# Output projection of a two-layer decoder: column blocks 2 and 3 done together, with two seven-product quads over the MLA heads

## The chip, the core and the metric

The kernel runs on one core of one Trainium2 chip. The metric is the device time of one execution in microseconds. Its engines are TensorE (PE in the profile, its weight loads PEld), VectorE (DVE), ScalarE (ACT), GpSimd (POOL) and SyncE (SP); loads are issued from SP's queue, accumulating transfers from GpSimd's.

## What is computed

Two layers over 256 tokens of width 2048. Each has a sparse attention (8 heads, "A") and an MLA attention (8 heads, "B") side by side, one output projection over both, a norm, and a SwiGLU FFN with a second norm. What the change touches is the last line of the mixer and the residual:

```
mix = einsum('bse,ed->bsd', concatenate([out_a, out_b], -1), w_o)   # 256 x 2048 by 2048 x 2048
x   = layer_norm(ALPHA * x + mix, ln1_g, ln1_b)
```

## The kernel before

Every product of fp32 data is made of three matmuls in a reduced fp32 format: both operands are split into a high and a low part (`split`, L427: ScalarE copies the high part, VectorE subtracts it for the low one), and high x high, high x low and low x high go into one PSUM bank (`proj`, L378, lines 392 to 394). Weights come in units of 256 rows by 512 columns (two 128-row pieces side by side, 128x1024 on chip, 512 KB): `load_raw` issues the load from SP's queue into one of four raw buffers, `parts` (L360) splits it into one of five pairs wh/wl. A unit serves both halves of the tokens (t = 0 and 1, 128 each) with two pieces and three matmuls, 12 matmuls of 128x512.

The projection's rows are 16 pieces: 0 to 7 are the A heads, 8 to 15 the B heads (`olhs`, L935). Its columns are four blocks of 512. For each block, `proj` runs over six units (`first`, L939: 8, 10, 12, 14, 0, 2), into two banks, one for each half of the tokens, and VectorE adds them into x (L944). The last two A units (4 and 6) are left for `last_pass` (L951): after the last attention heads it takes each half of the tokens over all four blocks, adds into x (L974), and as soon as a half is complete spawns its norm (`norm_T`: bn_stats L439, bn_aggr L441, a power on GpSimd L445, bnnb L451, normalization on ScalarE L460, transposes on PE, scaling on ScalarE L469, cast and low part on VectorE L472 and L473). Its eight units are split ahead, four of them into tiles named "many" and "own". The FFN's first matmuls need the first half's norm.

Beside the projection run, as generators that are stepped once a unit (`tick`), the last two sparse attention pairs (their outputs oA are split by VectorE) and `presums` (L844): sums of FFN weights on VectorE (tile q, L863 to L867), written back to HBM by GpSimd's queue for later. The FFN already uses a scheme of seven products for a 2x2 block of products (`gate_up`): sums and differences of weights on VectorE, and of activations ("few", "many"), in place of the eighth product.

There are eight PSUM banks: 0 to 3 for `acc`, 4 and 5 for transposes (`trp`), 6 and 7 as one pair (`att`). The framework's scheduler puts the instructions in their final order on each engine; each engine then runs in that order.

## Time and profile before

| | us |
|---|---|
| median of 3 runs | 2135.92 |
| lowest, highest | 2135.21, 2136.48 |
| profiled execution | 2134.82 |
| its span, first to last instruction | 2133.0 |

A row of the timeline has the start in us from the span's start, the duration, the engine, the line, the operation, output <- inputs, the shape and a count, and in brackets how long the engine had been idle and what ended that. Equal rows that follow each other are merged, so a duration with a count is that of the run. A row of the windows has the stretch, its length, and the busy time and number of instructions (x) of each engine. Layer 0's projection starts at 285 us, layer 1's at about 1347. Lines of the profile are those of the kernel before.

### The profile page before, as it was taken

The page shows a single profiled execution, that of the slowest core. Times are in us where ns is not written, and L with a number is a line of the kernel's source. Part 1 is how long each engine was busy: PE and PEld are TensorE (multiplying, and loading weights), DVE is VectorE, ACT ScalarE, POOL GpSimd, SP SyncE. Part 2 cuts the span into 40 slices and gives each one's busy share as a digit, 9 for nine tenths or more (in the row PEclk, how much of TensorE's full clock was granted, in tenths as well). Part 3 has the DMA queues.
Part 4 walks back from the last instruction along what each step waited for, and adds up shares of the span by engine and source line. Part 5 has one row for each costly group of instructions (what it writes and reads, how often), then busy time and mean ns, then how long its engine had stood idle before and what let it go on. Part 6 is the DMA issues. An engine that isn't in the chain of part 4 may idle for free.

```text
span 2133.0 us, 28390 instructions
## 1 busy us (share of the span) xinstructions
PE 2119.3 (99%) x9894; PEld 1760.1 (83%) x9894; DVE 1860.1 (87%) x2359; ACT 1334.7 (63%) x1714; POOL 330.9 (16%) x527
## 2 busy tenths in 40 slices
PE   9999999999999999999999999999999999999998
PEld 8888888888878888888888888888888888888886
DVE  7696776899999999999867976778999999999997
ACT  6556654766666666766655566547666666666773
POOL 1222220011111110110012232201111111110111
PEclk9999999999999999999999999999999999999999
DMA  8688888588888989987657889885989988988984
GB/s 311 207 298 292 309 298 309 183 239 263 247 257 272 286 279 291 281 264 254 217 172 247 302 292 290 324 279 186 253 258 243 289 262 276 285 277 292 282 300 118
DMA packets 175439, 564.49 MB, mean 265 GB/s; under 512 B 30928, under 2 KB 31232, under 8 KB 174656
## 3 DMA queue, kind: packets, MB, share of 16 engines
q1 hardware_dynamic: 110736, 398.38, 52.1%
q0 software_dynamic: 51600, 160.77, 29.4%
q10 hardware_dynamic: 12960, 3.54, 1.1%
q8 instruction: 77, 1.26, 0.2%
q14 instruction: 66, 0.54, 0.1%
HBM read 506.51 MB, written 31.46 MB: 252 GB/s over the span
## 4 chain that ended last, share of the span: by engine, by line
PE 88%; DVE 7%; issue 2%; DMA 1%; ACT 1%; POOL 0%; SPq 0%; DVEq 0%; ACTq 0%; POOLq 0%
PE acc L392 9%; PE acc L393 9%; PE acc L394 9%; PE acc L1186 7%; PE acc L1187 7%; PE acc L1185 7%; PE gu_p L1068 6%; PE gu_p L1071 6%; PE gu_p L1070 6%; DVE wl L429 3%; PE gu_c L1068 3%; PE gu_c L1071 3%; PE gu_c L1070 3%; PE tr L425 2%; PE att L1068 2%
## 5 line engine op out<-in xcount | busy, mean ns | idle before, releaser
L428 ACT ACTIVATE wh<-raw 128x1024 fp32r<-128x1024 f32 (+2 forms) x925 | 948.1, 1050 | 538.0 <-PE acc L394 128.1
L429 DVE TENSOR_TENSOR wl<-raw,wh 128x1024 fp32r<-128x1024 f32 (+2 forms) x925 | 1090.3, 1212 | 186.2 <-ACT wh L428 184.1
L392 PE MATMUL acc<-wh,xhl 128*128 128x512 f32 (+1 forms) x756 | 296.9, 393 | 0.0
L394 PE MATMUL acc<-wh,xhl 128*128 128x512 f32 (+1 forms) x756 | 292.1, 387 | 0.0
L393 PE MATMUL acc<-wl,xhl 128*128 128x512 f32 (+1 forms) x756 | 291.7, 386 | 0.0
L1186 PE MATMUL acc<-wl,hT 128*128 128x512 f32 x640 | 249.6, 390 | 0.9 <-DVE wl L429 0.8
L1185 PE MATMUL acc<-wh,hT 128*128 128x512 f32 x640 | 250.3, 392 | 0.0
L1187 PE MATMUL acc<-wh,hT 128*128 128x512 f32 x640 | 249.4, 390 | 0.0
L392 PEld LDWEIGHTS acc<-wh,xhl 128*128 128x128 f32 x756 | 142.0, 188 | 30.2 <-issue 3.3
L394 PEld LDWEIGHTS acc<-wh,xhl 128*128 128x128 f32 x756 | 141.9, 188 | 27.2
L393 PEld LDWEIGHTS acc<-wl,xhl 128*128 128x128 f32 x756 | 142.1, 188 | 26.5 <-DVE wl L429 1.2
L1186 PEld LDWEIGHTS acc<-wl,hT 128*128 128x128 f32 x640 | 120.2, 188 | 27.0 <-DVE wl L429 2.8
L1187 PEld LDWEIGHTS acc<-wh,hT 128*128 128x128 f32 x640 | 120.1, 188 | 25.1
L1185 PEld LDWEIGHTS acc<-wh,hT 128*128 128x128 f32 x640 | 120.2, 188 | 24.3
L1194 POOL DMA_DIRECT2D x<-d x80 | 68.1, 855 | 425.1 <-ACT d L1193 424.0
L1070 PE MATMUL gu_c<-wl,xhl 128*128 128x512 f32 x336 | 130.9, 390 | 0.1
L1071 PE MATMUL gu_c<-wh,xhl 128*128 128x512 f32 x336 | 130.7, 389 | 0.0
L1068 PE MATMUL gu_c<-wh,xhl 128*128 128x512 f32 x336 | 130.7, 389 | 0.0
L1193 ACT ACTIVATE d<-acc 128x512 f32<-128x512 f32 x80 | 47.7, 596 | 75.8 <-PE acc L1187 75.8
L1070 PE MATMUL gu_p<-wl,many 128*128 128x512 f32 x240 | 93.5, 390 | 0.0
L1068 PE MATMUL gu_p<-wh,many 128*128 128x512 f32 x240 | 93.4, 389 | 0.0
L1071 PE MATMUL gu_p<-wh,many 128*128 128x512 f32 x240 | 93.4, 389 | 0.0
(309 smaller groups left out, 3847.2 us busy)
## 6 DMA issues: line engine op xcount, KB each, us to landing
raw<-in_w_gate_dram SPq DMA_DIRECT2D x176, 512.0 KB, 5.6
raw<-in_w_down_dram SPq DMA_DIRECT2D x176, 512.0 KB, 8.2
raw<-in_w_in_dram SPq DMA_DIRECT2D x144, 512.0 KB, 5.6
sum<-in_w_up_dram POOLq DMA_DIRECT2D x124, 512.0 KB, 7.5
raw<-in_w_up_dram SPq DMA_DIRECT2D x100, 512.0 KB, 5.7
raw<-in_w_o_dram SPq DMA_DIRECT2D x64, 512.0 KB, 6.2
q<-q POOLq DMA_DIRECT2D x56, 512.0 KB, 5.0
raw<-q SPq DMA_DIRECT2D x56, 512.0 KB, 5.8
```

The lines of the kernel that those rows point to most:

```text
L392: mm(o[t][:, :n], h, a, start=first, stop=False)
L393: mm(o[t][:, :n], h, b, start=False, stop=False)
L394: mm(o[t][:, :n], l, a, start=False, stop=final)
L428: high = nc.scalar.activation(hi, src, AF.Copy)
L429: nc.vector.tensor_tensor(lo, src, f(hi), op=ALU.subtract)
L1068: mm(o[name], h, a, start=name not in begun, stop=False)
L1070: mm(o[name], h, b, start=False, stop=False)
L1071: mm(o[name], l, a, start=False, stop=end)
L1185: mm(o[c][t], h, wh[:, j, :], start=begin, stop=False)
L1186: mm(o[c][t], h, wl[:, j, :], start=False, stop=False)
L1187: mm(o[c][t], lo, wh[:, j, :], start=False, stop=end)
L1194: nc.gpsimd.dma_start(xt[t][:, c * C:(c + 1) * C], d, accum_op=ALU.add)
```

## The change

Blocks 0 and 1 go on as before. Blocks 2 and 3 become one stage, `col_pair`: first the A units 0 and 2 plainly for both blocks, into four banks (c11 and c21 are block 2's for the two token halves, c12 and c22 block 3's), then, once the attention is done, two quads. A quad takes the B units 8 and 12 (then 10 and 14), of both columns, for both token halves: seven products of six matmuls instead of eight. Four weight tiles r11, r12, r21, r22 are loaded; VectorE makes four sums of them in place; sums and differences of the heads' outputs (`head_sums`, spawned ahead of block 1) are the other operands. p6 and p7 get a transpose bank each, p1 and p5 the pair. After the second quad c22, c11, c12 and c21 go into x as before, the rest through four differences in small buffers, of which GpSimd's queue adds four into x by accumulating transfers.

```diff
+        places = ((8, 12), (10, 14))
+
+        def head_sums():
...
+            for u, v in places:
+                few = t8([P, 4, 2, KU, P], F32R, "hsum")
...
+                    nc.vector.tensor_tensor(w, f(hi), f(lo), op=ALU.add)
...
+                    nc.vector.tensor_tensor(w, y, z, op=ALU.subtract)
+                    split(few[:, i, 0], few[:, i, 1], w)
...
+                a21 = o(1, u)
+                s1 = diff(0, a21, o(1, v))
+                a11 = o(0, u)
+                s2 = diff(1, a11, s1)
+                diff(2, a21, a11)
+                diff(3, o(0, v), s2)
+                yield 1
...
+        def col_pair(cols, ks, sums):
...
+            finish(*a)
+            (c11, c21), (c12, c22) = (o[c] for c in cols)
+            p6, p7, p15 = trp(), trp(), att()
...
+            into(1, 1, c22)
+            for q, (u, v) in enumerate(places):
+                final = q == len(places) - 1
+                two = t8([P, 2, KU * C], F32, "wsum")
+                r11, r12 = two[:, 0], two[:, 1]
...
+                r21, r22 = (load_raw(w_o[l, c, v // KU], KU * C) for c in cols)
...
+                product(p1, token(0), r11, u, begin, final)
...
+                        nc.scalar.activation(e0, p1, AF.Copy)
+                product(c11, token(0), r21, v, False, final)
+                if final:
+                    into(0, 0, c11)
+                    added(0, 0, e0)
+                tick()
+                nc.vector.tensor_tensor(r12, r12, r22, op=ALU.add)
+                product(c12, summed("s4"), r22, u, False, final)
+                if final:
+                    into(0, 1, c12)
+                nc.vector.tensor_tensor(r11, r12, r11, op=ALU.add)
+                product(p6, summed("s2"), r11, u, begin, final)
+                if final:
+                    e1 = less(e0, p6)
+                tick()
+                nc.vector.tensor_tensor(r21, r11, r21, op=ALU.add)
+                product(p7, summed("s3"), r12, u, begin, final)
+                if final:
+                    e2 = less(e1, p7)
+                nc.vector.tensor_tensor(r22, r11, r22, op=ALU.subtract)
+                product(c21, token(1), r21, v, False, final)
+                if final:
+                    into(1, 0, c21)
+                    added(1, 0, e2)
+                tick()
+                product(p5, summed("s1"), r22, u, begin, final)
+                if final:
+                    for t, e in ((0, e1), (1, e2)):
+                        added(t, 1, less(p5, e))
+                tick()
...
-        for c in range(D // C):
+        for c in range(2):
+            if c:
+                spawn(held(head_sums(), head))
             o = proj([(w_o[l, c, k // KU], range(k, k + KU)) for k in first], olhs, C)
...
+        col_pair((2, 3), (0, 2), head)
+        turns["acc"] = 2
         finish(*a)
```

`into` is VectorE's scalar_tensor_tensor of ALPHA * x + bank (L1001 of the changed kernel), `less` its difference of two tiles or banks (L1006), `added` the accumulating transfer (L1010), `product` splits a weight tile and issues the six matmuls.

How the instructions move is shown at two places on VectorE in layer 0. The first is after block 0's eviction into x. Before, the rows are that eviction (x, acc), low parts of block 1's third to sixth units (wl), presums (q) and an attention output (oA):

```order
L944 SCALAR_TENSOR_TENSOR x1_66<-x1_66,acc658_2999 128x512
L944 SCALAR_TENSOR_TENSOR x2_67<-x2_67,acc659_3000 128x512
L429 TENSOR_TENSOR wl735_3286<-raw733_3283,wh734_3285 128x1024
L866 TENSOR_TENSOR q669_3045<-q673_3067,q669_3045 128x1024
L867 TENSOR_TENSOR q692_3125<-q673_3067,q692_3125 128x1024
L429 TENSOR_TENSOR wl738_3306<-raw736_3303,wh737_3305 128x1024
L429 TENSOR_TENSOR oA454_2189<-tr723_3235,oA453_2188 128x512
L429 TENSOR_TENSOR wl743_3328<-raw741_3325,wh742_3327 128x1024
L429 TENSOR_TENSOR wl748_3350<-raw746_3347,wh747_3349 128x1024
```

In the change the same eviction is followed by 24 small operations of the head sums (av, sv, hsum), with block 1's third unit, the two attention outputs and the presums among them; this is how that stretch ends, and the fourth unit's low part (wl756) stands behind it:

```order
L952 TENSOR_TENSOR av744_3298<-oB314_1589,oB315_1590 128x256
L866 TENSOR_TENSOR q669_3045<-q673_3067,q669_3045 128x1024
L429 TENSOR_TENSOR hsum737_3279<-sv742_3290,hsum737_3279 128x256
L957 TENSOR_TENSOR sv745_3300<-av744_3298,sv742_3290 128x256
L429 TENSOR_TENSOR oA454_2189<-tr750_3326,oA453_2188 128x512
L429 TENSOR_TENSOR hsum737_3279<-sv745_3300,hsum737_3279 128x256
L867 TENSOR_TENSOR q692_3125<-q673_3067,q692_3125 128x1024
L429 TENSOR_TENSOR wl756_3356<-raw754_3353,wh755_3355 128x1024
L429 TENSOR_TENSOR wl761_3378<-raw759_3375,wh760_3377 128x1024
```

Block 1's fourth unit (wl738 before, wl756 now) has moved from the sixth row to behind 31 rows.

The second place is the end of the blocks 2 and 3. Before, it is the last units of block 3, the weights of the last pass (own, wl) and the evictions:

```order
L429 TENSOR_TENSOR wl788_3574<-raw786_3571,wh787_3573 128x1024
L429 TENSOR_TENSOR wl793_3599<-raw791_3596,wh792_3598 128x1024
L429 TENSOR_TENSOR own799_3616<-raw803_3623,own799_3616 128x1024
L429 TENSOR_TENSOR wl797_3609<-raw795_3606,wh796_3608 128x1024
L429 TENSOR_TENSOR own804_3627<-raw808_3634,own804_3627 128x1024
```

In the change it is the second quad: weight sums (wsum, and raw in place), low parts of its products (wl), a weight of the last pass (many), evictions (L1001) and differences (we):

```order
L1050 TENSOR_TENSOR wsum803_3578<-wsum803_3578 128x1024
L429 TENSOR_TENSOR many826_3680<-raw830_3687,many826_3680 128x1024
L1055 TENSOR_TENSOR raw804_3581<-wsum803_3578,raw804_3581 128x1024
L1001 SCALAR_TENSOR_TENSOR x1_66<-x1_66,acc767_3417 128x512
L429 TENSOR_TENSOR wl814_3623<-wsum803_3578,wh813_3622 128x1024
L1001 SCALAR_TENSOR_TENSOR x1_66<-x1_66,acc769_3419 128x512
L429 TENSOR_TENSOR wl817_3636<-wsum803_3578,wh816_3635 128x1024
L1006 TENSOR_TENSOR we815_3632<-we808_3595,tr783_3493 128x512
L1059 TENSOR_TENSOR raw805_3583<-wsum803_3578,raw805_3583 128x1024
L1006 TENSOR_TENSOR we818_3645<-we815_3632,tr784_3494 128x512
L429 TENSOR_TENSOR wl820_3649<-raw804_3581,wh819_3648 128x1024
L429 TENSOR_TENSOR wl822_3661<-raw805_3583,wh821_3660 128x1024
```

The last pass's splits, but for one "many", have moved behind the quad's products.

## Prediction

> **What bounds the kernel now.** I read the page first (engines, then the slices), then the waits of PE, then PE's and VectorE's timeline at the output projection of layer 0, then the windows there.

> ```profile
> span 2133.0 us, 28390 instructions
> PE 2119.3 (99%) x9894; PEld 1760.1 (83%) x9894; DVE 1860.1 (87%) x2359; ACT 1334.7 (63%) x1714; POOL 330.9 (16%) x527
> ```

> And who PE itself waited for (us in total, times, longest):

> ```profile
> PE acc L200 <- POOL ident masks.py:199: 1.6, 1, 1.6
> PE acc L1186 <- DVE wl L429: 0.8, 1, 0.8
> ```

> PE is fed nearly all the time: its longest recorded wait after the start is 0.8 us. But its 99% overstates how full it is, since the recorded 0.39 us of a matmul overlap with the next one. What a matmul costs is the distance from one start to the next.

> ```profile
> 316.47 0.39 PE L392 MATMUL acc<-wh,oB 128*128 128x512 f32 x1
> 316.70 0.39 PE L393 MATMUL acc<-wl,oB 128*128 128x512 f32 x1
> ...
> 319.19 0.39 PE L392 MATMUL acc<-wh,oA 128*128 128x512 f32 x1
> ```

> The first and the last row are twelve matmuls apart, the whole of one weight unit: 2.72 us, 0.2267 us each. VectorE (DVE) is the other full engine, 87% over the span. In the output projection it is less full, and that is the room the change works in. How much room there is in layer 0:

> ```profile
> 304.50:325.00 20.50, 20.50 (x102) 17.27 (x101) 13.56 (x15) 9.14 (x12) 2.67 (x5) 1.00 0.89 327
> 325.00:345.00 20.00, 20.00 (x90) 16.57 (x89) 13.78 (x15) 10.17 (x10) 1.21 (x2) 1.00 1.02 334
> 345.00:371.00 26.00, 26.00 (x116) 21.52 (x115) 18.53 (x23) 10.05 (x10) 0.56 (x1) 1.00 0.79 294
> ```

> The columns after the length are PE, PE's weight loads, VectorE, ScalarE, GpSimd, then granted clock, DMA share and GB/s. VectorE is busy 13.56 + 13.78 + 18.53 = 45.9 of 66.5 us, so 20.6 us are free. DMA is full (1.02) in the middle stretch.

> **PE's saving.** Two column blocks over the eight MLA heads' 128-row pieces take 4 units x 2 columns x 12 = 96 matmuls; two quads of seven products of six take 84. Two layers save 24 x 0.2267 = 5.4 us. By the 0.39 us of a row it would look like 9.4; the spacing decides.

> **VectorE's bill, per layer.** Per-instruction prices, from starts that follow each other without a gap:

> ```profile
> 304.49 1.27 DVE L944 SCALAR_TENSOR_TENSOR x<-x,acc 128x512 f32<-128x512 f32 x2
> 305.69 1.21 DVE L429 TENSOR_TENSOR wl<-raw,wh 128x1024 fp32r<-128x1024 f32 x1
> 306.82 1.21 DVE L866 TENSOR_TENSOR q<-q,q 128x1024 f32<-128x1024 f32 x1
> 307.96 1.21 DVE L867 TENSOR_TENSOR q<-q,q 128x1024 f32<-128x1024 f32 x1
> ```

> The same for the small sums that the FFN makes of its activations, and for the norm's statistics:

> ```profile
> 424.10 0.42 DVE L429 TENSOR_TENSOR few<-sv,few 128x256 fp32r<-128x256 f32 x1
> 424.43 0.42 DVE L1012 TENSOR_TENSOR sv<-av,sv 128x256 f32<-128x256 f32 x1
> 424.77 1.22 DVE L1128 TENSOR_TENSOR raw<-sum,raw 128x1024 f32<-128x1024 f32 x1
> ```

> ```profile
> 364.52 0.70 DVE L439 BATCH_NORM_STATS2 bnst<-x 128x6 f32<-128x512 f32 x1
> 365.13 0.67 DVE L974 SCALAR_TENSOR_TENSOR x<-acc,x 128x512 f32<-128x512 f32 x1
> ```

> A 128x1024 costs 1.135 us, a 128x512 0.60, a 128x256 0.335, a bn_stats 0.61. Added: six more weight splits (fourteen products against eight units) 6.8, eight weight sums 9.1, twenty-four small head sums, differences and low parts 8.0, four differences of banks 2.4; the four evictions into x replace four. That is 26.3 us against 20.6 free: it doesn't fit, by 5.7 us, even if VectorE never waits again. The head's sums also add eight small ScalarE operations and the six high parts, some 10 us, but ScalarE is busy only 9 to 10 of each 20 us there.

> [...] The sum goes by the spacing.

> **From the bill to the end.** VectorE runs in order, and I follow its queue from the eviction of column block 0 to the instruction that releases the norm of the first 128 tokens (bnnb, L451), because the FFN's first matmuls need that norm.

> ```profile
> 370.94 0.16 DVE L451 SCALAR_TENSOR_TENSOR bnnb<-bnmv,bnrs 128x1 f32<-128x1 f32 x1 [0.68 <-POOL bnrs L445]
> ...
> 371.14 2.94 ACT L460 ACTIVATE x<-x,bnnb,bnrs 128x512 f32<-128x512 f32 x4 [0.36 <-DVE bnnb L451]
> 373.98 1.04 ACT L428 ACTIVATE wh<-raw 128x1024 fp32r<-128x1024 f32 x1
> ...
> 376.95 1.51 ACT L469 ACTIVATE v<-tr,gbT 128x128 f32<-128x128 f32 x4 [0.69 <-PE tr L425]
> ...
> 378.77 0.41 DVE L472 CAST xhl<-v 128x512 fp32r<-128x512 f32 x1
> ...
> 380.32 0.48 PE L392 MATMUL acc<-wh,xhl 128*128 128x512 f32 x1
> ...
> 1365.89 1.27 DVE L944 SCALAR_TENSOR_TENSOR x<-x,acc 128x512 f32<-128x512 f32 x2
> ...
> 1432.71 0.16 DVE L451 SCALAR_TENSOR_TENSOR bnnb<-bnmv,bnrs 128x1 f32<-128x1 f32 x1 [0.68 <-POOL bnrs L445]
> ...
> 1442.08 0.48 PE L392 MATMUL acc<-wh,xhl 128*128 128x512 f32 x1
> ```

> Now this stretch takes 66.45 us (304.49 to 370.94) in layer 0 and 66.82 in layer 1. In the change VectorE's order has between the same two instructions 43 of 128x1024, 21 of 128x512, 24 of 128x256, five bn_stats and three tiny ones: 43 x 1.135 + 21 x 0.60 + 24 x 0.335 + 5 x 0.61 + 0.5 = 73.0 us without one gap. So bnnb comes at least 6.55 us later in layer 0, 6.2 in layer 1.

> Not all of that reaches PE. Today 9.4 us pass from bnnb to the first FFN matmul (380.32), and part of it is ScalarE splitting two weights in between and PE finishing the second half's pass. The bare chain is 0.2 + 2.84 (four normalizations) + 1.82 (four scalings and their handoff to the cast) + about 0.5 (cast and handoff), 5.4 us, and in the change's order ScalarE has no split between these steps. So 4.0 us are absorbed and the FFN starts 2.55 and 2.2 us later: **+4.8 us is the floor**, if VectorE never waits. The 2.72 us that PE saves a layer lie inside this: PE reaches the FFN early and stands there, or stands earlier, at the places below.

> VectorE will wait. The new small operations stand ahead of the low part of block 1's fourth unit (first place shown above). Its end is 304.49 + 2 x 0.60 + 24 x 0.335 + 4 x 1.135 + 2 x 0.60 = 319.5, where PE now begins that unit at 316.47; PE can do the few matmuls that need only the high part, then stands some 2 us. That split also frees the raw buffer into which the first unit of block 3 is loaded (raw has four buffers, given out in turn). Loads of that kind, with the median and then the bounds of the time to landing, and ScalarE's wait for one of them (total, times, longest):

> ```profile
> raw<-in_w_o_dram SPq DMA_DIRECT2D x64, 512.0 KB, 6.2
> ```

> ```profile
> DMA to landing us min/median/max: 3.4/6.2/12.7
> ```

> ```profile
> ACT many L428 <- DMA raw<-in_w_o_dram: 13.0, 3, 7.3
> ```

> Landing takes 3.4 us at best and 6.2 in the median; then ScalarE's high part, 1.05 us. VectorE has three splits meanwhile (to 322.9) and can go on at 319.5 + 6.2 + 1.05 = 326.7: 3.8 us idle. Between 1.1 (shortest) and more than that (the longest is 12.7) I take the median, since DMA is as full there as now. The second stall place is the last quad: PE needs a product's low part each 6 x 0.2267 = 1.36 us, while VectorE there has seven splits, four sums, one split for the last pass and eight 128x512 for 9.5 us of PE: 12 x 1.135 + 8 x 0.6 = 18.4. PE stands there several times.

> Sum: (2.55 + 3.8) + (2.2 + 3.8) = 12.35 us. The profiled execution took 2134.82, so 2147.2; the median of the runs is 2135.92, 1.1 above it, so about **2148**.

> Costed at nothing: the four accumulating DMAs a layer (256 KB) on GpSimd's queue. GpSimd does 0.56 us in 345 to 371, and what stands behind them, the power for bnrs (L445), needs VectorE's bn_aggr, which is later anyway. The last pass reads the x that they add to some 10 us later in VectorE's queue; if they landed later than that, each microsecond would delay the norm by as much. The loads into wsum are the same bytes as before.

> **Rivals.**
> (a) *The lead hides it: faster.* VectorE runs ahead of PE by up to five split buffers; if the free 20.6 us and that lead covered the bill, the FFN would start 2.72 us earlier a layer: 2135.9 - 5.4 = 2130.5. For: PE has hardly waited for VectorE so far. Against: at 304.49 only two of block 1's units are split ahead, and the queue's own length fixes bnnb. It decides if VectorE's work between the two instructions is 66.45 + 4.0 - 2.7 = 67.7 us or less rather than 73. Chance 0.05.
> (b) *VectorE hardly waits.* The loads land in time, and the floor holds: 2135.9 + 4.8 = 2140.7. For: loads in this stretch can land in 3.4 us. Against: DMA at 1.02. Chance 0.14, half of it within 0.2%.
> (c) *ScalarE blocked by the last pass's weights.* In the change ScalarE's high part of a "many" weight stands ahead of the high parts of quad products. The row above shows ScalarE waiting up to 7.3 us for such a load; today a lead covers that. If 3 to 5 us a layer of it show up, 2155 to 2158. For: the burst of loads when the next phase's buffers open comes later now, and nearer to the use. Against: in PE's order the products concerned come some 10 us after the loads can start. Chance 0.14.

> **The numbers.** The forecast (VectorE-bound, some 2144 to 2153) has 0.67. The range goes from just under the floor (2140) to the end of (c), 2158. A measurement of this kernel can tell about 0.2% from no change (4.3 us): faster 0.05, same 0.07 (half of b), slower 0.88.

> **What would show it.** Right: in the profile after, VectorE has almost no idle time from the first head sum to bnnb, bnnb lies 73 to 79 us after block 0's eviction, and PE waits for VectorE's wl (L429) in block 1, in the last quad and at the FFN's start, about 9 us a layer in all. Wrong: bnnb less than 68 us after the eviction, or PE without waits in the quads (then a); VectorE idle on ScalarE for more than 6 us a layer, with ScalarE waiting on a "many" load (then c). A stall moved into the FFN's seven-product quads, where VectorE is full today, would make it slower than (c).

## The result and the profile after

The changed kernel takes 2165.65 us (median of 4 runs, 2164.06 to 2166.23), the kernel before 2135.85 beside it: 1.0141 times as long, 95% interval 1.0129 to 1.0153, so +29.8 us where +12 was predicted. The profiled execution took 2166.23. First the page's engines, then what PE waited for (us in total, times, longest):

```profile
span 2164.5 us, 28489 instructions
PE 2128.6 (98%) x9870; PEld 1762.1 (81%) x9870; DVE 1910.4 (88%) x2443; ACT 1351.9 (62%) x1744; POOL 341.0 (16%) x535
```

```profile
PE tr L1025 <- ACT wh L428: 5.8, 2, 3.6
PE acc L392 <- DVE xhl L472: 4.6, 2, 2.3
PE acc L393 <- DVE wl L429: 4.3, 2, 2.3
PE att L1025 <- ACT wh L428: 3.4, 2, 1.9
```

PE, which before never waited longer than 0.8 us past the start, now waits in the quads (tr and att are the banks of p6, p7, p1 and p5), in block 1 (L393) and at the FFN's start (L392), once a layer each. The largest wait is for ScalarE's high part. VectorE's timeline from block 0's eviction to bnnb, and the FFN's first matmul:

```profile
304.74 1.27 DVE L1082 SCALAR_TENSOR_TENSOR x<-x,acc 128x512 f32<-128x512 f32 x2
...
326.88 2.48 DVE L429 TENSOR_TENSOR wl<-raw,wh 128x1024 fp32r<-128x1024 f32 x2 [3.68 <-ACT wh L428]
...
345.40 1.23 DVE L429 TENSOR_TENSOR wl<-wsum,wh 128x1024 fp32r<-128x1024 f32 x1 [5.13 <-ACT wh L428]
...
389.85 0.15 DVE L451 SCALAR_TENSOR_TENSOR bnnb<-bnmv,bnrs 128x1 f32<-128x1 f32 x1
...
395.58 0.50 PE L392 MATMUL acc<-wh,xhl 128*128 128x512 f32 x1 [2.32 <-DVE xhl L472]
...
1382.73 1.27 DVE L1082 SCALAR_TENSOR_TENSOR x<-x,acc 128x512 f32<-128x512 f32 x2
...
1404.01 2.48 DVE L429 TENSOR_TENSOR wl<-raw,wh 128x1024 fp32r<-128x1024 f32 x2 [2.68 <-ACT wh L428]
...
1425.48 1.23 DVE L429 TENSOR_TENSOR wl<-wsum,wh 128x1024 fp32r<-128x1024 f32 x1 [4.08 <-ACT wh L428]
...
1465.49 0.15 DVE L451 SCALAR_TENSOR_TENSOR bnnb<-bnmv,bnrs 128x1 f32<-128x1 f32 x1
```

The stretch takes 85.11 us in layer 0 (389.85 - 304.74) and 82.76 in layer 1, where 73.0 without a gap was worked out. All idle times in the brackets of the stretch's rows add up to 11.42 and 8.94; without them it is 73.7 and 73.8. The second large gap of each layer has its cause on ScalarE:

```profile
343.37 1.06 ACT L428 ACTIVATE many<-raw 128x1024 fp32r<-128x1024 f32 x1 [8.51 <-DMA raw<-in_w_o_dram]
344.33 1.04 ACT L428 ACTIVATE wh<-wsum 128x1024 fp32r<-128x1024 f32 x1
...
1423.44 1.06 ACT L428 ACTIVATE many<-raw 128x1024 fp32r<-128x1024 f32 x1 [8.29 <-DMA raw<-in_w_o_dram]
```

ScalarE waits over 8 us for a weight that only the last pass needs, and the high part of a summed quad weight (wh<-wsum), which VectorE and PE wait for, stands right behind it. This is the rival (c). What PE does after that wait:

```profile
342.89 0.39 PE L1027 MATMUL acc<-wh,hsum 128*128 128x512 f32 x1
345.42 0.50 PE L1025 MATMUL tr<-wh,hsum 128*128 128x512 f32 x1 [2.14 <-ACT wh L428]
...
347.27 0.63 PE L1027 MATMUL tr<-wh,hsum 128*128 128x512 f32 x1
347.70 0.63 PE L1025 MATMUL tr<-wh,hsum 128*128 128x512 f32 x1
...
352.39 0.63 PE L1027 MATMUL acc<-wh,oB 128*128 128x512 f32 x1
352.82 0.44 PE L1025 MATMUL acc<-wh,oB 128*128 128x512 f32 x1
353.10 0.39 PE L1026 MATMUL acc<-wl,oB 128*128 128x512 f32 x1
```

From 347.27 on the matmuls last 0.63 us instead of 0.39 and start 0.43 apart instead of 0.227: PE's clock has fallen. The windows show it in the granted clock (0.80; everywhere in this stage before: 1.00) and VectorE nearly full from there on:

```profile
325.00:345.00 20.00, 17.92 (x77) 13.90 (x75) 12.91 (x12) 7.89 (x8) 1.74 (x2) 1.00 1.00 333
345.00:371.00 26.00, 22.06 (x71) 16.38 (x72) 23.86 (x25) 16.97 (x19) 1.69 (x2) 0.80 0.50 161
371.00:395.00 24.00, 22.26 (x105) 18.31 (x103) 23.45 (x32) 11.55 (x18) 3.17 (x3) 1.00 0.83 268
```

In the whole execution the trace records half the clock in five stretches behind stalls, 23.9 us in all. Some 44 matmuls (give or take two, by how the edges are counted) run 0.20 us slower each in them, 8.8 us of PE time; before there is none. Where the time lies, from PE's rows ("stage": first output-projection matmul to first FFN matmul of a layer):

| | stage, layer 0 | stage, layer 1 | FFN 0 to stage 1 | FFN 1 to the end |
|---|---|---|---|---|
| before | 95.11 | 95.47 | 966.29 | 690.92 |
| changed | 110.12 | 108.01 | 967.63 | 693.28 |

15.0 and 12.5 of the span's 31.5 us are in the two stages, 3.7 behind the two FFN starts.

### The profile page after: what moved, and what is told of

Its sections match the earlier page's. It is cut to its first block, busy times and chain, and to the rows that moved or that the text cites. A ratio compares the mean times of both kernels' runs of the same rounds, so it can differ in the third digit from the quotient of the medians.

```text
span 2164.5 us, 28489 instructions
## 1 busy us (share of the span) xinstructions
PE 2128.6 (98%) x9870; PEld 1762.1 (81%) x9870; DVE 1910.4 (88%) x2443; ACT 1351.9 (62%) x1744; POOL 341.0 (16%) x535
## 4 chain that ended last, share of the span: by engine, by line
PE 83%; DVE 9%; issue 4%; DMA 2%; ACT 1%; POOL 0%; SPq 0%; DVEq 0%; ACTq 0%; POOLq 0%
PE acc L392 7%; PE acc L394 7%; PE acc L393 7%; PE acc L1326 7%; PE acc L1327 7%; PE acc L1325 7%; PE gu_p L1211 6%; PE gu_p L1208 6%; PE gu_p L1210 6%; DVE wl L429 4%; PE gu_c L1211 3%; PE gu_c L1208 3%; PE gu_c L1210 3%; PE tr L425 2%; PE att L1211 2%
## 5 line engine op out<-in xcount | busy, mean ns | idle before, releaser
L428 ACT ACTIVATE wh<-raw 128x1024 fp32r<-128x1024 f32 (+2 forms) x925 | 948.1, 1050 | 543.8 <-PE acc L394 114.2
L429 DVE TENSOR_TENSOR wl<-raw,wh 128x1024 fp32r<-128x1024 f32 (+2 forms) x925 | 1089.5, 1210 | 174.9 <-ACT wh L428 172.5
L392 PE MATMUL acc<-wh,xhl 128*128 128x512 f32 (+1 forms) x756 | 298.3, 395 | 4.6 <-DVE xhl L472 4.6
L393 PE MATMUL acc<-wl,xhl 128*128 128x512 f32 (+1 forms) x756 | 292.5, 387 | 0.0
L392 PEld LDWEIGHTS acc<-wh,xhl 128*128 128x128 f32 x756 | 142.6, 189 | 35.3 <-DVE xhl L472 5.1
L393 PEld LDWEIGHTS acc<-wl,xhl 128*128 128x128 f32 x756 | 142.7, 189 | 26.4 <-DVE wl L429 1.2
## 6 DMA issues: line engine op xcount, KB each, us to landing
raw<-in_w_gate_dram SPq DMA_DIRECT2D x176, 512.0 KB, 5.5
raw<-in_w_down_dram SPq DMA_DIRECT2D x176, 512.0 KB, 7.8
raw<-in_w_in_dram SPq DMA_DIRECT2D x144, 512.0 KB, 5.7
sum<-in_w_up_dram POOLq DMA_DIRECT2D x124, 512.0 KB, 7.3
raw<-in_w_up_dram SPq DMA_DIRECT2D x100, 512.0 KB, 5.8
q<-q POOLq DMA_DIRECT2D x56, 512.0 KB, 4.6
raw<-in_w_o_dram SPq DMA_DIRECT2D x56, 512.0 KB, 5.9
raw<-q SPq DMA_DIRECT2D x56, 512.0 KB, 6.0
```

The source lines that it names most:

```text
L392: mm(o[t][:, :n], h, a, start=first, stop=False)
L393: mm(o[t][:, :n], h, b, start=False, stop=False)
L428: high = nc.scalar.activation(hi, src, AF.Copy)
L429: nc.vector.tensor_tensor(lo, src, f(hi), op=ALU.subtract)
```

## The experiments

The expectations call the theories by number. Theory 1, on which the prediction was built: VectorE's total of work sets the time. Theory 2: ScalarE, held by the load of a "many" weight, holds up the quads' high parts behind it (from here on "the block"). Theory 3: PE's clock falls after a stall, and that adds to it. Theory 4: the column pair costs by itself. Theories 5 and 6 came out of later runs and are told in the expectations of experiments 8 to 10. The explanation to be tested was theory 2 with 3, against 1 and 4. Each ratio is to the kernel before on the same chip (2134.8 to 2136.1 in these runs).

**1. The last pass's high parts behind the quads'.**

```diff
-                us.append([load_unit(...), parts(load_raw(...), KU * C, own)])
+                with (tc.issue_after(held) if held is not None else ExitStack()):
+                    us.append([load_unit(...), parts(load_raw(...), KU * C, own)])
...
-        last_pass(..., olhs, then, 1.0)
+        last_pass(..., olhs, then, 1.0, held=latest["high"])
```

> Only the place of four ScalarE instructions a layer changes: the high parts of the last pass's weights (many, own) stand behind the high part of the last quad product instead of among the quads' high parts. Nothing is left out. Theory 1, VectorE's work alone (its queue is longer by the 26.3 us a layer that the prediction counts): the work is the same, so the time stays within 2 us of the changed kernel, 2164 to 2168. Theory 2, ScalarE blocked by a load: the waits of VectorE behind many (5.1 us in layer 0, 4.1 in layer 1) go, so 2155 to 2158. Theory 3, PE's clock falls after a stall: it adds to theory 2, since the 2.3 us stall at 343.1 and the slow matmuls behind it (some 15 x 0.2 us) go too: 2150 to 2154.

2148.95 us, 1.0063 (1.0048 to 1.0078): 16.7 us are gained without any work of the program being taken away, a little more than theories 2 and 3 together were given. 15 slow matmuls are left of 44, and the stages take 100.96 and 100.03 us. Theory 1 alone falls as the explanation of the 29.8. But 12.9 us over the kernel before remain. VectorE's stretch in layer 0 is 75.10 us with 5.00 idle:

```profile
305.07 1.27 DVE L1082 SCALAR_TENSOR_TENSOR x<-x,acc 128x512 f32<-128x512 f32 x2
```

(bnnb, at 380.17, is shown with experiment 9.) That is near the forecast's 73.0 and 3.8, but not the same work: VectorE's order followed the edit, and two 128x1024 and two 128x512 operations a layer left the stretch, so 70.1 us of work are in it, not 73.7.

**2. Without the heads' sums.**

```diff
-                    return lambda k: sums[name, k]
+                    return lambda k: olhs(name in ("s3", "s4"), k)
...
-                spawn(held(head_sums(), head))
```

> Left out: the sums of the MLA heads' activations (24 small VectorE and 8 small ScalarE operations a layer); the products that need them take a plain operand instead. PE's work, the weights' sums and all loads stay. Theory 1: VectorE's bill falls by 8.0 us a layer to 65.0, below the 67.7 from which it decides, and the 3.8 us wait in block 1 goes: 2130 to 2140. Theory 2: the wait behind many stays, 4 to 5 us a layer: 2142 to 2150. Theory 3: if that stall stays, the slow matmuls behind it stay too, so the upper end of theory 2 or above.

2159.87 us, 1.0113 (1.0098 to 1.0128), only 5.8 less, and above what theories 1 and 2 were given. The edit moved more than it should: VectorE's order in block 0 is another, and PE waits there for the softmax, a wait that the changed kernel doesn't have:

```profile
PE att L834 <- DVE lg L573: 7.8, 2, 4.0
```

It says little on the sums. Experiment 4 is the cleaner form.

**3. The column pair plainly; 6. the same with early evictions.** Both leave out the quads, with their sums and differences; the line that calls the pair, and what 6 adds:

```diff
-        col_pair((2, 3), (0, 2), head)
+        col_pair((2, 3), (0, 2, 8, 10, 12, 14), head)
...
 # 6, in the loop over the columns
+                    if i == len(ks) - 1:
+                        for t in range(NT):
+                            sl = xt[t][:, c * C:(c + 1) * C]
+                            with tc.high_priority(offset=SOONER):
+                                nc.vector.scalar_tensor_tensor(sl, sl, ALPHA, o[c][t], op0=ALU.mult, op1=ALU.add)
```

> The column pair is kept (columns 2 and 3 together in four banks, evicted at the end), but all six unit rows are multiplied plainly: no seven products, no sums of weights or heads, no differences of banks, 24 more matmuls in all than the changed kernel. The result is the full one. Theories 1 and 2 (the cost is VectorE's and ScalarE's work for the seven products): as the kernel before, 2134 to 2139. Rival theory 4, the pair itself costs (four banks held, all evictions at the end, loads in another order): 2142 to 2160.

> The plain column pair again (six unit rows for both columns, no seven products), with the evictions of a column issued right behind its last unit and ahead in priority, as the changed kernel does it. Nothing is left out. In the plain pair before it PE waited 7.4 us for evictions that stood behind weight splits in VectorE's queue. If that was its whole cost (11.5 us over the kernel before): 2135 to 2139. If holding four banks and loading the columns in turn costs by itself (theory 4): it stays at 2144 to 2149.

2147.57 us (1.005, 1.0034 to 1.0067), then 2144.78 (1.0042, 1.0028 to 1.0056): theory 4 holds in part. Four banks that are finished together leave the last pass none to start in, and their evictions stand in VectorE's queue behind weight splits:

```profile
PE acc L1028 <- DVE x L991: 7.4, 3, 4.3
```

The priority helps little: 6.3 us of this wait remain. But it isn't the changed kernel's cost: there the quads' evictions come one by one, and the last pass waits for no bank.

**4. The heads' sums from block 0 on.**

```diff
-            if c:
+            if not c:
                 spawn(held(head_sums(), head))
```

> The heads' sums are made from column block 0 on instead of block 1; nothing else moves by intent and nothing is left out. VectorE has gaps of 3.5, 1.1, 1.5, 1.5 and 1.5 us between 278 and 296 in the changed kernel's profile, 9.1 us, for 8.0 us of sums. Theory 1: the bill in the stretch falls by 8.0 us a layer and the wait of 2.5 us in block 1 goes: 2142 to 2150. Theory 2: the wait behind many stays and takes back most of it: 2150 to 2160. Theory 3: as theory 2, with PE's slow matmuls still there after a stall over 2 us.

2149.55 us, 1.0062 (1.0047 to 1.0077): 16.1 us, nearly the whole of what experiment 1 gained, from the other side. The waits in block 1 are gone (L393 no longer shows), and 14 slow matmuls are left. The number is at the upper end of theory 1's range. It doesn't set the theories apart, because the block shrank too: ScalarE's wait in front of the first "many" is 3.63 us in layer 0 and 7.46 in layer 1, where it was 8.51 and 8.29.

**5. Both edits together** (the diffs of 1 and 4).

> The two earlier edits together: the last pass's high parts behind the last quad product's (gained 16.7 us alone) and the heads' sums made from column block 0 on (gained 16.1 alone). Nothing is left out. If both only shorten one VectorE queue between the eviction of block 0 and bnnb (theory 1 with theory 2's gap in it): its bill is then 73.0 - 8.0 = 65.0 us without a gap, below the 67.7 from which it no longer decides, so the FFN starts no later than in the kernel before and up to 2.7 us a layer earlier: 2131 to 2138. If both mend the same stall (the load behind which many waits, and the slow matmuls behind the stall): the gains don't add, 2145 to 2149.

2147.12 us, 1.0056 (1.0043 to 1.007). The gains don't add: with one edit made, the other brings about 2 us. VectorE's work in the stretch is 7 us smaller than in experiment 1 (62.9 against 70.1), yet the stretch is 74.01 us instead of 75.10 in layer 0 (and 74.93 instead of 73.78 in layer 1), and its idle time in layer 0 rose from 5.00 to 11.10. The saved work has turned into waiting. The windows show where:

```profile
305.00:325.00 20.00, 19.72 (x98) 16.41 (x97) 14.34 (x19) 9.62 (x13) 2.65 (x5) 1.00 0.93 344
325.00:345.00 20.00, 18.76 (x82) 14.90 (x81) 15.06 (x15) 9.44 (x9) 1.74 (x2) 1.00 0.76 249
345.00:371.00 26.00, 22.88 (x94) 16.84 (x93) 25.44 (x28) 16.21 (x17) 3.39 (x4) 1.00 0.62 166
```

VectorE is free for 5 us in each of the first two windows and then full, 25.44 of 26. It can't do the later work earlier: ScalarE's rows show that it waits for PE to give a split buffer back, and VectorE for it:

```profile
323.32 1.06 ACT L428 ACTIVATE wh<-raw 128x1024 fp32r<-128x1024 f32 x1 [1.71 <-PE acc L394]
326.04 1.06 ACT L428 ACTIVATE wh<-wsum 128x1024 fp32r<-128x1024 f32 x1 [1.66 <-PE acc L394]
```

**7. Ten more matmuls in the wait ahead of the FFN.**

```diff
+        spare = bank((turns["acc"] + 1) % 4, "acc")
+        for _ in range(10):
+            mm(spare, x, w, start=True, stop=True)
```

> The changed kernel with ten more matmuls a layer between the last transposes of the norm and the first FFN matmul, into the bank that the FFN then starts afresh; the order of VectorE, ScalarE, GpSimd and SyncE is the same, and nothing is left out. PE idles 2.3 us there in both layers today, and 7 and 5 matmuls at a spacing of 0.43 us follow about 4 us later. The ten take 10 x 0.2267 = 2.27 us. Theory 3 (an idle PE lowers its clock a little later): the slow matmuls at 397 to 400 and 1472 to 1475 are gone, those behind the other stalls stay, and the time falls by up to 12 x 0.2 = 2.4 us: 2163 to 2165. If the clock falls for another reason: the slow matmuls stay and the time is 2165 to 2167.

In the changed kernel the FFN's matmuls run slow some 2 us after that wait:

```profile
397.39 0.63 PE L393 MATMUL acc<-wl,xhl 128*128 128x512 f32 x1
...
399.95 0.63 PE L394 MATMUL acc<-wh,xhl 128*128 128x512 f32 x1
```

With the wait filled, none does, in either layer:

```profile
390.00 2.54 PE L1130 MATMUL acc<-own,oA 128*128 128x512 f32 x10
392.64 0.47 PE L392 MATMUL acc<-wh,xhl 128*128 128x512 f32 x1
...
400.02 0.39 PE L392 MATMUL acc<-wh,xhl 128*128 128x512 f32 x1
```

So an idle PE is the cause of the slow matmuls behind it (theory 3). The rows show that, the time doesn't: 2165.33 us (1.0139, 1.0125 to 1.0153) falls into the range that was set for another reason (2165 to 2167), by 0.33 us, and the 2.4 us don't appear. In the profiled execution 0.9 instead of 3.7 us lie behind the FFN starts, but the stages took 2.7 more, with the softmax holding PE for 2.1 us in layer 1 and slow matmuls elsewhere (some 41 in all). What the clock costs in total isn't settled to better than the 8.8 us of PE time.

**8. The plain units between the quads; 9. one quad only** (both on experiment 5's kernel).

```diff
 # 8: first quad, then plainly(), then the second quad
+                if final:
+                    plainly()
+                    into(1, 1, c22)
 # 9
-        places = ((8, 12), (10, 14))
+        places = ((10, 14),)
...
-        col_pair((2, 3), (0, 2), head)
+        col_pair((2, 3), (0, 2, 8, 12), head)
```

> The two edits together as before (last pass's high parts late, heads' sums early), and the column pair in another order: first quad, then the two plain unit rows, then the second quad. Nothing is left out and the work of every engine is the same. In the two edits together VectorE sat idle some 10 us between 314 and 337, waiting for ScalarE, which waits for PE to give back one of five split buffers, and is then busy 25.4 of 26 us from 345 to 371. Theory 5 (VectorE's free time before the quads can't be saved up for them, so what counts is its work between the first quad and the norm): 11 us of plain matmuls between the quads, for which VectorE has four splits (4.5 us), give it 6 us of room there, and the time falls to 2132 to 2141. Theory 1 (VectorE's total in the stretch): the same work, so 2145 to 2149.

> The two edits together, but only heads 10, 11, 14 and 15 as a quad of seven products; heads 8, 9, 12 and 13 plainly in the column pair. Nothing is left out. PE does 12 matmuls more in all than the changed kernel (2.7 us), VectorE some 10 us less in a layer, half of what the quads added. Theory 5: the work between the quad and the norm is what counts, and most of the pile-up before the last pass stays: 2138 to 2145. Theory 1: the bill is far below the point where it decides, 2133 to 2137.

2144.37 us (1.0046, 1.0034 to 1.0059) and 2156.49 (1.0102, 1.0086 to 1.0117): theory 5's numbers are missed by both, by 3 and 11 us. Experiment 8 never ran at half clock inside the kernel (mean granted clock of the profiled execution: 0.999), so the clock isn't what keeps it above the kernel before. In the second, part is again a wait for the softmax in block 0 (2.6 and 3.3 us). So its time is no clean price of a quad; but half the added work gone, and no gain, is instructive. VectorE's first sum of the only quad, bnnb and the FFN:

```profile
345.31 1.23 DVE L1046 TENSOR_TENSOR wsum<-wsum,raw 128x1024 f32<-128x1024 f32 x1 [3.20 <-DMA raw<-in_w_o_dram]
...
382.15 0.16 DVE L451 SCALAR_TENSOR_TENSOR bnnb<-bnmv,bnrs 128x1 f32<-128x1 f32 x1 [0.46 <-POOL bnrs L445]
...
388.49 0.50 PE L392 MATMUL acc<-wh,xhl 128*128 128x512 f32 x1 [1.66 <-DVE xhl L472]
```

36.8 us from one to the other, with 0.67 idle; in experiment 1 the last quad's first sum and bnnb stand 36.3 apart, with 0.39 idle, and in experiment 8 35.7:

```profile
343.91 1.22 DVE L1046 TENSOR_TENSOR wsum<-wsum,raw 128x1024 f32<-128x1024 f32 x1
...
380.17 0.16 DVE L451 SCALAR_TENSOR_TENSOR bnnb<-bnmv,bnrs 128x1 f32<-128x1 f32 x1
```

The last quad and the last pass make a tail of VectorE work without a gap; experiment 9's VectorE was idle for 17 us ahead of it, to no use. That made theory 6.

**10. Both quads first, the plain units behind them** (with both edits).

```diff
-            for i, k0 in enumerate(ks):          # the plain units
-                for c in cols:
...
             for q, (u, v) in enumerate(places):
...
+            for i, k0 in enumerate(ks):
+                for c in cols:
...
+                    if i == len(ks) - 1:
+                        for t in range(NT):
+                            into(t, c - cols[0], o[c][t])
+            added(0, 0, e0)
...
```

> The two edits together, and the column pair in a third order: both quads first, then the two plain unit rows; the four evictions into x stand at the end, the differences of banks behind the second quad, the adding transfers behind the evictions. Nothing is left out. Theory 6 (from the second quad's first weight sum to bnnb VectorE has a tail of 36 us or more with under 1 us idle, whatever was saved before, and the FFN starts 42 to 43 us behind that sum at best; what counts is when that tail begins and how long it is): the quads' weights come some 15 us earlier in the queue and 11 us of plain matmuls lie behind them, for 4.5 us more of splits in the tail, so PE becomes the bound again: 2129 to 2137. If VectorE's total in the stretch counts (theory 1): the same work, 2143 to 2148. Against a gain: the adding transfers come at the end, beside the last pass, and each us by which they land late costs one.

2131.51 us (11 runs), 0.9988 (0.9979 to 0.9997): 3.8 us under the kernel before, 34 under the changed one. It is the only version below the kernel before, and barely clear of the noise: two of the 11 runs (2136.53 and 2137.77) lie above it. Its profile, engines, then PE's waits past the start:

```profile
span 2129.5 us, 28488 instructions
PE 2114.8 (99%) x9870; PEld 1756.4 (82%) x9870; DVE 1910.0 (90%) x2443; ACT 1352.7 (64%) x1744; POOL 352.8 (17%) x535
```

```profile
PE tr L425 <- DVE oA L429: 0.9, 2, 0.6
PE acc L1324 <- DVE wl L429: 0.8, 1, 0.8
```

```profile
305.44 1.27 DVE L1079 SCALAR_TENSOR_TENSOR x<-x,acc 128x512 f32<-128x512 f32 x2
...
320.41 1.22 DVE L1031 TENSOR_TENSOR wsum<-wsum,raw 128x1024 f32<-128x1024 f32 x1
...
373.17 0.16 DVE L451 SCALAR_TENSOR_TENSOR bnnb<-bnmv,bnrs 128x1 f32<-128x1 f32 x1
```

VectorE's busy time is that of the changed kernel (1910.0 against 1910.4). The last quad's first sum comes at 320, not 344 as in experiment 1; the stretch takes 67.73 us with 1.90 idle, and not one matmul is slow.

**11, 12. Without the weight sums of the first quad, of the second** (both on experiment 5's kernel, quads last).

```diff
+                if q == 1:     # 12: q == 0
                     nc.vector.tensor_tensor(r12, r12, r22, op=ALU.add)
 ...
```

> The two edits together, and the four weight sums of the first quad are left out in each layer (its products take the raw weights): 4 x 1.135 = 4.5 us of VectorE a layer less. Theory 6: they lie before the tail, where VectorE idles some 10 us anyway, so at most 1 to 2 us of the 2147: 2144 to 2148. Theory 1: 4.5 us a layer come off the time, 2138 to 2140.

> The same with the four weight sums of the second quad left out instead of the first's: again 4.5 us of VectorE a layer less, but inside the tail. Theory 6: the tail is 4.5 us shorter, so 2137 to 2141. Theory 1: the same as leaving out the first quad's, 2138 to 2140; the two theories differ in the difference between these two runs, 5 to 10 us against none.

2142.51 us (1.0035, 1.0023 to 1.0047) and 2137.55 (1.0013, 1.0004 to 1.0022): 4.6 and 9.6 us under 2147.12. The same 9.1 us of work in two layers is worth about twice as much inside the tail as ahead of it; the runs of each kernel spread over 6 us, and the two intervals just don't meet. By theory 1 they would be equal. Theory 6 had the second right; the first gained 1.5 us more than it allowed. Leaving the sums out also spares ScalarE the waits for them (in experiment 1 3.92 and 3.06 us for two of the second quad's in layer 0), which these runs don't tell from VectorE's saving.

**13, 14. Experiment 10's order without the two edits, and with the heads' sums early alone** (its diff on the changed kernel, and with the diff of 4).

> The changed kernel with the order of the column pair alone changed: both quads first, then the two plain unit rows. The heads' sums stay in block 1, the last pass's high parts stay among the quads' on ScalarE. Nothing is left out. If the quads' place at the end was the cause and the block and the sums only showed there: 2131 to 2138. If the ScalarE block costs by itself: it now stands earlier, 2 to 5 us a layer and the slow matmuls behind it come back: 2140 to 2155, with PE waiting on wh in the quads.

> The same order of the pair with the heads' sums made from block 0 on; the last pass's high parts stay among the quads'. Nothing is left out. It differs from the best version (2131.5) only in the place of four ScalarE instructions a layer. If the block costs by itself: 2136 to 2146. If it needs the quads to stand last: 2130 to 2134. The difference to the run beside it is what the heads' sums in block 1 cost: 0 to 8 us.

2153.7 us (1.0088, 1.0072 to 1.0105) and 2143.98 (1.0044, 1.0029 to 1.0059). The block costs by itself: 12.5 us between experiments 14 and 10, which differ in the edit of experiment 1 alone. The heads' sums in block 1 cost 9.7 us between 13 and 14, more than the 0 to 8 expected. The row of experiment 13 shows it standing earlier, with quad products' high parts behind it:

```profile
329.48 1.06 ACT L428 ACTIVATE many<-raw 128x1024 fp32r<-128x1024 f32 x1 [3.03 <-DMA raw<-in_w_o_dram]
330.45 1.99 ACT L428 ACTIVATE wh<-wsum 128x1024 fp32r<-128x1024 f32 x2
```

All versions with two quads of seven products side by side:

| quads | neither edit | sums early | high parts late | both |
|---|---|---|---|---|
| last | 2165.65 | 2149.55 | 2148.95 | 2147.12 |
| first | 2153.70 | 2143.98 | not run | 2131.51 |

With the quads last, either edit reaches a floor near 2148, the tail; with the quads first the floor is gone, the sums early bring 9.7 us, and the high parts late 12.5 more.

## Why the prediction was wrong

The direction was right; the size, 12.35 us against 29.8, was short by 17.5.

- *PE's saving, 5.4 us.* Right as a bound: only experiment 10 shows any of it, with stages of 93.23 and 94.00 us, 3.35 less together than before.
- *VectorE's bill, 73.0 us in the stretch.* Right: 73.7 and 73.8 without idle time, so the spacing's 1.135 us was the price to take.
- *From bnnb to the FFN, 4.0 us absorbed.* Right: 5.73 us against 9.38, 3.65 absorbed.
- *PE's stall in block 1 and the wait behind it.* Right: PE 2.05 and 2.26 us; VectorE 3.68 and 2.68, predicted 3.8.
- *The accumulating transfers at nothing.* Right: no row of VectorE in the stage waits for them.
- *The step that failed* is the term for VectorE's idle time: 3.8 us a layer, where 11.42 and 8.94 were measured, 12.8 too little in all. 5.13 and 4.08 of it is rival (c); with the block moved, in experiment 1, layer 0 is idle for 5.00 us, 4.17 of it block 1's wait. The rival was priced well (3 to 5) but set against the forecast as another case with a chance of 0.14, though both could happen and did. What spoke against it in the text, that the products come 10 us after the loads can start, failed: ScalarE waited 8.5 and 8.3 us for such a load. The seven w_o loads issued from 328 to 337 us took 11.1 us in the median to land, where the median of the kernel before was 6.2. The sign set for (c) came: VectorE idle on ScalarE for 9.07 and 7.06 us (block 1's wait is in it), more than 6, and ScalarE waiting on a "many" load. And the rival's end, 2158, left out PE's clock, which no term of the prediction held.
- *The rest:* 3.7 us lie behind the FFN's starts, which the sum took to be shifted and nothing else. In experiment 7, where the slow matmuls there are gone, it is 0.9. With the idle time's 12.8, this 3.7, the bill's 1.5 over 73.0, 0.7 less absorbed and a start 0.25 later the sum of 12.35 becomes 31.3; the spans differ by 31.5.
- *The reasoning behind the floor* was wrong, and that experiment 1 came to 2148.95, beside the forecast's 2148, is in part luck. It took the stretch as one account, in which free time before can pay for work later. Against experiment 1, experiments 5 and 9 took 7 and 13 us a layer from that account (62.9 and 56.8 us of work in layer 0, where 70.1 were); the first gained 2 us, the second lost time. 11 and 12 showed that the place of a saving counts, and 10 moved it below 2136 with no work taken away. Only there, with hardly an idle gap, does the account hold: stretches of 67.73 and 67.53 us, at the 67.7 from which rival (a) was to decide, and 2131.51 where it gave 2130.5.

Open: why the saving of experiment 10 is 3.8 us and not 5.4 (its labelled waits in the stages are 0.9), and how much of the 16.7 us of experiment 1 is the wait and how much the clock. Its 29 slow matmuls fewer are an estimated 5.8 us of PE time at 0.20 each, so the wait is likely the larger part.

## What to carry to other kernels

Before adding work to an engine because it has free time, ask whether that time can be saved up: here five split buffers were the whole lead (in experiment 5 ScalarE waited 1.71 and 1.66 us for one of them), and work at the end of a stage had to be done at the end. Put the products that cost the second engine most first, and the plain ones, where it catches up, last: here that order took 2147.12 us to 2131.51. And look along the in-order queue of each engine for an instruction whose data come late and are needed late, with one behind it that is needed now: here ScalarE stood 8.51 us in front of a "many", and moving such instructions back gained 16.7 us.

## What the runs showed of the hardware

```profile
342.67:346.08 3.41, 1.11 (x4) 0.37 (x2) 0.68 (x1) 2.71 (x3) 0.00 (x0) 1.00 1.03 420
346.08:352.90 6.82, 6.22 (x15) 4.86 (x16) 6.75 (x7) 6.82 (x8) 0.00 (x0) 0.50 0.43 152
...
1393.97:1397.38 3.41, 1.75 (x8) 1.13 (x6) 3.41 (x4) 0.00 (x0) 0.83 (x2) 1.00 0.25 100
1397.38:1400.80 3.42, 2.83 (x12) 2.37 (x13) 3.42 (x4) 0.00 (x0) 0.23 (x1) 1.00 0.99 295
```

The first lies in one window, which leaves PE idle for 2.30 us, and the clock is halved in the next. The second, though longer, is cut by the edge of a window into 1.66 and 0.59 us of idle time, and the clock stays. By the recorded busy time, over all 16 traces up to 2110 us, 9836 windows of the grid were at full clock: the half clock followed on all 20 with 1.95 us of idle time or more, on 9 of the 19 from 1.5 to 1.95, and on none of the 9797 below 1.5. Short waits add up in it: in experiment 13 two of 0.44 and 0.90 us, in a window with 1.51 us of idle time, were enough.
